# Two mixer blocks on one core: slab columns taken later and freed sooner, and four constants loaded into the slab for their stage

## The chip, the cores and the metric

The kernel runs on one core of a Trainium2 chip. The metric is the device time of one execution in microseconds (us). The engines are TensorE (PE in the profile, with its weight loads as PEld), VectorE (DVE), ScalarE (ACT), GpSimd (POOL) and SyncE (SP), which here only issues transfers. All run at the same time, each through its own instructions in a fixed order, and wait for one another on semaphores.

## What is computed

Two transformer blocks over 256 tokens of width 1024, in 32-bit floats. The part that matters here is the first block's mixer:

```python
hn = rms_norm(h, norm_mix_pre)
p = hn @ w_in                                   # 6912 columns
p_rw, p_ret, g_rw, g_ret = split(p)
y_rw  = rwkv7_mixer(p_rw, ...)                  # recurrence over the tokens, 8 heads of 64
y_ret = retention_mixer(p_ret, positions)       # 8 heads, decay mask, silu gate, group norm
merged = sigmoid(g_rw) * (y_rw @ w_branch_rw) + sigmoid(g_ret) * (y_ret @ w_branch_ret)
h = h + rms_norm(merged @ w_out, norm_mix_post)
```

After it come a convolutional feed-forward layer and the second block (a gated feed-forward layer, a gated mixer with a state-space branch, another feed-forward layer and an output gate).

## The kernel before, in words

**Weights.** All weights come as one stream of 335 chunks of 128 x 1024 floats (512 KB). A chunk is loaded by SP into one of six `stage` buffers, split by ACT into an f16 part (`hi`) and by DVE into the bf16 remainder (`lo`), and then used by PE in three products for each 128 x 128 tile (hi x hi, hi x lo, lo x hi). `take` (class `Stream`) loads five chunks and splits two chunks ahead of use. A chunk is 24 products of 256 columns, or 12 of 512 columns where the tokens are the stationary side (`token_major`). A product goes to a PSUM bank, `main` for the stream and `side` for the mixers' small products; the bank is free for the next tile when ACT or DVE has read it.

**The slab.** Everything else lives in one SBUF tensor, `slab`, of 32688 columns of 128 floats. `pr.buf(n)` takes n columns (class `Slab`), `.free()` gives them back. Columns that are given back are taken again later in the program, and then the new owner's first write must wait until the old owner's last reader or writer is done: a wait between two steps that have no data in common. `Slab.get` looks for a place whose old owner is done early, by the times of the plan's last round, and takes a later one where there is none.

**The order of the work.** The program is run once to record every operation with its operands (`Plan.add`, `Plan.touch`); a list scheduler (`Plan.run`) then gives each engine its order by its own prices, and `build` repeats this for four rounds and keeps the one with the shortest plan. `Plan.issue` emits the instructions in that order, so nearly all of them have line 484 in the profile. The order on each engine is fixed from then on: an instruction that waits holds up all that stand behind it on its engine.

**The first block's mixer.** `BlockOne.run` (lines 1539 to 1672) streams `w_in`: first the columns of RWKV, then retention's v, q and k, retention's gate (`RET_G`, four tiles of 512 columns, read from PSUM by `evac_g`, line 1517), and the two branch gates (16 tiles, `evac_gate`, line 1524). Beside it run two generators, `rwkv` (line 1059) and `retention` (line 1427), that hand in their small steps between the stream's tiles. `rwkv` builds decayed keys and queries for four tiles t, then

- writes the diagonal blocks of its triangular matrices to HBM and reads them back by rows into `lt` (lines 1225 to 1232),
- inverts them by forward substitution, 31 steps of two DVE operations on `x`, `tmp` and `lt` (lines 1246 to 1259),
- writes the result to HBM twice (`scr_g`, `scr_h`) and reads it back into `gb`, `hb` and `rb`, which must be zero elsewhere (lines 1222 to 1224 and 1260 to 1274),
- multiplies the blocks together (lines 1280 to 1304), solves for the state in two halves, and normalizes (lines 1307 to 1400).

`retention` works on four heads at a time (a quad): scores, decay mask, product with v, statistics; then the gate and eight transposes that give `y_ret`. The branches' products follow in the stream: `w_branch_ret` needs all of `y_ret`, `w_branch_rw` all of `y_rw`.

**The constants in question.** `w2a2` and `g2` (512 columns each, second half of `cst`), `sel8t` and `eye32` (512 each, in `konst`) are loaded at the start into tensors of their own and stay for the whole program. `decay` (3072 columns) and retention's v (`vrb`, 2048) are slab buffers, taken before retention begins and freed after it has ended.

Of the kernel before, what the change touches and what calls it, by code (L numbers as in the profile page):

```python
# [18 lines left out]
T = 256  # L19
# [29 lines left out]
SLAB = 32688  # L49
# [946 lines left out]
class BlockOne:  # L996
# [64 lines left out]
    def rwkv(self):  # L1061
# [3 lines left out]
        w2a2, g2 = pr.col("w2a2", 0, 512), pr.col("g2", 0, 512)  # L1065
# [36 lines left out]
        for t in range(4):  # L1102
# [31 lines left out]
            mm(bank[:, 0:T], lhsT=k_["sel8t"][:, t * P : t * P + P], rhs=rk.ap, start=True, stop=True)  # L1134
# [83 lines left out]
        rk.free()  # L1218
        self.wdad.free()


        gb, hb, rb = pr.buf(1024), pr.buf(2048), pr.buf(512)
        for b in (gb, rb, hb):
            pr.G.memset(b.ap, 0.0)
# [25 lines left out]
        V.tensor_copy(x.ap, k_["eye32"])  # L1250
# [8 lines left out]
        V.tensor_copy(tmp.v("p (c i) -> p i c", c=16), xv)  # L1259
        sg = pr.dram("scr_g", (2, 4, 16, 32, 16))  # L1260
        sh = pr.dram("scr_h", (2, 4, 16, 16, 32))
        pr.plan.sync.dma_start(out=sg.rearrange("a b h i c -> (a b h) (i c)"), in_=x.ap)
        pr.plan.sync.dma_start(out=sh.rearrange("a b h c i -> (a b h) (c i)"), in_=tmp.ap)
        hcs = lambda b: b.v("p (h n) -> p h n", h=16)
# [10 lines left out]
        for b in (lt, x, tmp):  # L1275
            b.free()
# [97 lines left out]
        for b in (u, ut, b2, state, hb, m4, r0, vt, bt, kt0, *self.AR, *self.F):  # L1374
            b.free()
        rs = pr.buf(16)
# [10 lines left out]
        for t in range(4):  # L1387
            bank = pr.bank()
            for c in range(2):
                pr.transpose(bank[:, c * P : c * P + P], ytv[:, c, t * P : t * P + P])  # L1390
            mm(bank[:, T : 2 * T], lhsT=g2[:, t * P : t * P + P], rhs=self.gd.ap, start=True, stop=True)
            o = pr.buf(T)
            S.activation(o.ap, bank[:, 0:T], AF.Identity, scale=pr.col("rw_lnx_w", t), bias=pr.col("rw_lnx_b", t))
            V.tensor_tensor(out=o.ap, in0=o.ap, in1=self.bv[t].ap, op=ADD)
            V.tensor_tensor(out=o.ap, in0=bank[:, T : 2 * T], in1=o.ap, op=MUL)
            self.bv[t].free()
            pr.unbank(bank)
            self.y_rw.append(pr.split(o.ap))
            o.free()
            yield  # L1400
        yt.free()
        self.gd.free()
# [25 lines left out]
    def retention(self):  # L1428
# [3 lines left out]
        for quad in range(2):  # L1432
# [5 lines left out]
            qs, kk = self.rot["q", quad], self.rot["k", quad]  # L1438
            for pair in range(2):
# [6 lines left out]
                for i, bank in enumerate(banks):  # L1446
                    h = 4 * quad + 2 * pair + i
                    s = pr.buf(384)
                    V.tensor_tensor(out=s.ap, in0=bank[:, 0 : 3 * P], in1=pr.k["decay"][:, 3 * P * h : 3 * P * h + 3 * P], op=MUL)
                    pr.unbank(bank)  # L1450
                    ss.append(s)
# [3 lines left out]
                for i, s in enumerate(ss):  # L1455
                    h = 4 * quad + 2 * pair + i
                    e = slice(P * i, P * i + P)
                    v0, v1 = self.vr[:, 0, h * P : h * P + P], self.vr[:, 1, h * P : h * P + P]
# [7 lines left out]
            for b in qs + kk:  # L1466
                b.free()
# [10 lines left out]
        self.vrb.free()  # L1478
# [34 lines left out]
    def evac_v(self, c, nh, ps):  # L1513
        self.pr.S.activation(self.vr[:, c, 512 * nh : 512 * nh + 512], ps, AF.Copy)
# [15 lines left out]
    def run(self):  # L1530
# [49 lines left out]
        dec = pr.buf(3072)  # L1580
        pr.plan.sync.dma_start(out=dec.ap, in_=pr.ins["decay"])
        pr.k["decay"] = dec.ap
        self.vrb = pr.buf(2048)
        self.vr = self.vrb.v("p (c n) -> p c n", c=2)
# [21 lines left out]
        dec.free()  # L1606
# [474 lines left out]
_KEEP = ("ones", "ident", "sel2", "sel8t", "inv", "mask", "blk64", "eye32")  # L2081


def build(tc, ins, out, at, at2):
    nc = tc.nc
    with tc.tile_pool(name="sb", bufs=1) as sb, \
# [7 lines left out]
        cst = sb.tile([P, ins["cst"].shape[1]], F32, name="cst")  # L2094
# [18 lines left out]
def program(pr, hall, kt):  # L2113
# [21 lines left out]
    load("sel2", "sel8t", "inv")  # L2135
    pr.plan.sync.dma_start(out=pr.cst[:, nv:], in_=ins["cst"][:, nv:])
    pr.ws.load_to(3)
    load("mask", "blk64", "eye32")
# [36 lines left out]
```

## Time and profile before

| | us |
|---|---|
| median of 3 runs (lowest, highest) | 1011.3 (1009.15, 1011.61) |
| the profiled execution | 1015.67 |
| its span, first to last instruction | 1013.9 |
| PE busy, PE idle in the span | 983.4, 30.5 |
| DVE busy | 794.5 |
| ACT busy | 613.8 |

The profiled execution is one run, 4.4 us above the median; the trace's times are counted from its first instruction. PE's granted clock is given as a share of 2.4 GHz: 1.00 is that level and 0.50 is 1.2 GHz. A pipelined product is shown longer than the step from one to the next (a product of 256 columns of f16 is shown with 270 ns), so where PE is full the records overlap and the busy time is that of their union. Since almost every instruction has line 484, groups are told apart by their operands: `lo<-stage,hi` is a split, `slab<-slab` on DVE with 496, 480, 464 ... columns is forward substitution, `slab<-main 128x512` on ACT is `evac_g` (or retention's v), `scr_l`, `scr_g` and `scr_h` are the three trips through HBM.

### The profile page before, as it was taken

The page shows a single profiled execution, that of the slowest core. Times are in us where ns is not written, and L with a number is a line of the kernel's source. Part 1 is how long each engine was busy: PE and PEld are TensorE (multiplying, and loading weights), DVE is VectorE, ACT ScalarE, POOL GpSimd, SP SyncE. Part 2 cuts the span into 40 slices and gives each one's busy share as a digit, 9 for nine tenths or more (in the row PEclk, how much of TensorE's full clock was granted, in tenths as well). Part 3 has the DMA queues.
Part 4 walks back from the last instruction along what each step waited for, and adds up shares of the span by engine and source line. Part 5 has one row for each costly group of instructions (what it writes and reads, how often), then busy time and mean ns, then how long its engine had stood idle before and what let it go on. Part 6 is the DMA issues. An engine that isn't in the chain of part 4 may idle for free.

```text
span 1013.9 us, 22086 instructions
## 1 busy us (share of the span) xinstructions
PE 983.4 (97%) x8884; PEld 830.6 (82%) x8899; DVE 794.5 (78%) x1515; ACT 613.8 (61%) x1042; POOL 34.6 (3%) x35
## 2 busy tenths in 40 slices
PE   8999996999998999999999999999999999999996
PEld 6766745998987888889888888768887888888884
DVE  7999698679888999756977756589798987776654
ACT  6774432545686877556655545577899665554543
POOL 2100000100001000000000000000000000000000
PEclk9899998999999999999999999999999999999999
DMA  9646656246636766664766666655545686666621
GB/s 344 233 150 197 183 166 194 74 155 224 204 96 220 218 203 204 204 197 140 236 204 204 200 198 205 198 179 161 198 124 173 201 273 205 202 196 205 198 75 42
DMA packets 60790, 189.68 MB, mean 187 GB/s; under 512 B 13184, under 2 KB 14992, under 8 KB 60176
## 3 DMA queue, kind: packets, MB, share of 16 engines
q1 hardware_dynamic: 59824, 185.39, 58.6%
q10 hardware_dynamic: 864, 2.89, 0.8%
q8 instruction: 69, 1.13, 0.5%
q14 instruction: 33, 0.27, 0.1%
HBM read 185.35 MB, written 1.85 MB: 185 GB/s over the span
## 4 chain that ended last, share of the span: by engine, by line
PE 71%; DVE 15%; ACT 6%; DMA 4%; issue 3%; POOL 1%; SPq 0%; POOLq 0%; ACTq 0%; DVEq 0%
PE main L484 44%; PE side L484 27%; DVE slab L484 11%; DVE lo L484 4%; ACT slab L484 3%; ACT hi L484 1%; DMA stage<-stream 1%; DMA slab<-scr_cs 1%; PE side L237 1%; DVE h L484 1%; POOL slab L484 1%; ACT L484 1%; DMA slab<-scr_l 1%; DMA h<-xt 1%; DMA scr_cs<-slab 0%
## 5 line engine op out<-in xcount | busy, mean ns | idle before, releaser
L484 PE MATMUL main<-slab,hi 128*128 128x256 f16 (+2 forms) x3276 | 553.7, 270 | 11.9 <-DVE slab L484 10.3
L484 PEld LDWEIGHTS <-hi 128*128 128x128 f16 x5080 | 489.3, 99 | 73.4 <-issue 13.3
L484 ACT ACTIVATE hi<-stage 128x1024 f16<-128x1024 f32 (+1 forms) x338 | 351.8, 1047 | 277.2 <-PE main L484 172.1
L484 DVE TENSOR_TENSOR lo<-stage,hi 128x1024 bf16<-128x1024 f32 (+1 forms) x338 | 406.8, 1210 | 139.3 <-ACT hi L484 138.5
L484 PE MATMUL main<-slab,lo 128*128 128x256 f16 (+1 forms) x1638 | 438.5, 272 | 0.4 <-DVE lo L484 0.4
L484 PE MATMUL side<-slab,hi 128*128 128x256 f16 (+3 forms) x1804 | 278.4, 260 | 2.0 <-DVE slab L484 1.1
L484 PEld LDWEIGHTS <-lo 128*128 128x128 bf16 x2540 | 249.2, 98 | 33.2 <-issue 3.7
L484 PE MATMUL side<-slab,lo 128*128 128x256 f16 (+1 forms) x902 | 225.3, 262 | 0.0
L484 DVE TENSOR_TENSOR slab<-slab 128x256 f32<-128x256 f32 (+13 forms) x427 | 165.5, 405 | 18.0 <-ACT slab L484 15.6
L484 ACT ACTIVATE slab<-slab 128x256 f32<-128x256 f32 (+4 forms) x302 | 116.7, 419 | 34.1 <-DVE slab L484 25.1
L484 PE MATMUL main<-hi,slab 128*128 128x512 f16 (+3 forms) x304 | 83.4, 357 | 0.6
L484 PEld LDWEIGHTS <-slab 128*128 128x128 f16 (+1 forms) x521 | 47.8, 101 | 42.6 <-issue 3.0
L484 ACT ACTIVATE slab<-side 128x128 f32<-128x128 f32 (+5 forms) x93 | 32.1, 379 | 51.8 <-PE side L484 42.5
L484 PEld LDWEIGHTS side<-slab 128*128 128x128 f32 x376 | 51.8, 192 | 8.4 <-DVE slab L484 4.4
L484 PE MATMUL side<-slab 128*128 128x64 f32 (+3 forms) x379 | 56.1, 264 | 2.5 <-DVE slab L484 2.3
L484 POOL TENSOR_TENSOR slab<-slab 128x2 f32<-128x2 f32 (+2 forms) x19 | 28.9, 1518 | 838.5 <-DVE slab L484 825.7
L484 PE MATMUL main<-lo,slab 128*128 128x512 bf16 (+3 forms) x138 | 48.5, 354 | 0.0
L484 DVE TENSOR_TENSOR slab<-side,slab 128x512 f32<-128x512 f32 (+4 forms) x58 | 32.7, 579 | 11.0 <-PE side L484 5.4
L484 DVE SCALAR_TENSOR_TENSOR slab<-main,cst,slab 128x255 f32<-128x255 f32 (+2 forms) x88 | 38.8, 469 | 1.6 <-ACT slab L484 1.5
L484 DVE SCALAR_TENSOR_TENSOR slab<-h,cst,slab 128x256 bf16<-128x256 f32 (+2 forms) x88 | 35.4, 427 | 2.3 <-ACT slab L484 2.2
L484 ACT ACTIVATE slab<-main 128x256 f32<-128x256 f32 (+2 forms) x66 | 25.3, 402 | 15.3 <-DMA scr_g<-slab 6.9
L484 DVE TENSOR_TENSOR slab<-main,slab 128x256 f32<-128x256 f32 (+1 forms) x53 | 28.6, 550 | 5.7 <-PE main L484 4.2
(60 smaller groups left out, 400.9 us busy)
## 6 DMA issues: line engine op xcount, KB each, us to landing
stage<-stream SPq DMA_DIRECT2D x332, 512.0 KB, 4.3
slab<-scr_cs SPq DMA_DIRECT2D x1, 2048.0 KB, 9.3
stage<-stream SPq DMA_DIRECT2D x6, 256.0 KB, 5.5
slab<-decay SPq DMA_DIRECT2D x1, 1536.0 KB, 8.4
slab<-slab SPq DMA_DIRECT2D x32, 32.0 KB, 1.9
slab<-last ACTq DMA_DIRECT2D x1, 1024.0 KB, 7.0
slab<-cst ACTq DMA_DIRECT2D x1, 1024.0 KB, 11.2
h<-xt SPq DMA_DIRECT2D x3, 256.0 KB, 6.1
```

What stands on the lines that cost most here:

```text
L237: op = self.new("PE", lambda: [fn(*args, **kw) for _, fn, args, kw in calls], (), {})
L484: o.fn(*o.args, **o.kw)
```

## The change

- The slab grows by 2048 columns to 34736, which are the columns of the four constants, no longer in `cst` and `konst`.
- `w2a2` and `sel8t` are loaded into slab buffers that `rwkv` takes as it begins and frees after its four tiles; `g2` into one that it takes near its end; `eye32` straight into `x`, in place of a DVE copy.
- `gb`, `hb` and `rb` (3584 columns) are taken after forward substitution instead of before it, and `lt` (1024) is freed before them instead of after.
- `decay` and v are held for each quad: two buffers of 1536 columns, taken as the quad begins, and two of 1024, each freed with its quad.

```diff
-SLAB = 32688
+SLAB = 34736
...
-        w2a2, g2 = pr.col("w2a2", 0, 512), pr.col("g2", 0, 512)
+
+        w2a2b, selb = pr.buf(512), pr.buf(512)
+        a = pr.at["w2a2"][0]
+        pr.plan.sync.dma_start(out=w2a2b.ap, in_=pr.ins["cst"][:, a : a + 512])
+        pr.plan.sync.dma_start(out=selb.ap, in_=pr.ins["sel8t"])
+        w2a2 = w2a2b.ap
...
-        rk.free()
+        for b in (rk, selb, w2a2b):
+            b.free()
         self.wdad.free()
-
-
-        gb, hb, rb = pr.buf(1024), pr.buf(2048), pr.buf(512)
-        for b in (gb, rb, hb):
-            pr.G.memset(b.ap, 0.0)
...
-        V.tensor_copy(x.ap, k_["eye32"])
+        pr.plan.sync.dma_start(out=x.ap, in_=pr.ins["eye32"])
         for j in range(31):
...
         V.tensor_copy(tmp.v("p (c i) -> p i c", c=16), xv)
+        lt.free()
         sg = pr.dram("scr_g", (2, 4, 16, 32, 16))
...
         pr.plan.sync.dma_start(out=sh.rearrange("a b h c i -> (a b h) (c i)"), in_=tmp.ap)
+
+
+        gb, hb, rb = pr.buf(1024), pr.buf(2048), pr.buf(512)
+        for b in (gb, rb, hb):
+            pr.G.memset(b.ap, 0.0)
...
-        for b in (lt, x, tmp):
+        for b in (x, tmp):
             b.free()
...
+        g2b = pr.buf(512)
+        a = pr.at["g2"][0]
+        pr.plan.sync.dma_start(out=g2b.ap, in_=pr.ins["cst"][:, a : a + 512])
         rs = pr.buf(16)
...
+            dec = pr.buf(1536)
+            pr.plan.sync.dma_start(out=dec.ap, in_=pr.ins["decay"][:, 1536 * quad : 1536 * quad + 1536])
             for pair in range(2):
...
-            for b in qs + kk:
+            for b in (*qs, *kk, dec, self.vrb[quad]):
                 b.free()
...
-        self.vrb.free()
...
-        dec = pr.buf(3072)
-        pr.plan.sync.dma_start(out=dec.ap, in_=pr.ins["decay"])
-        pr.k["decay"] = dec.ap
-        self.vrb = pr.buf(2048)
-        self.vr = self.vrb.v("p (c n) -> p c n", c=2)
+        self.vrb = [pr.buf(1024) for _ in range(2)]
+        self.vr = [b.v("p (c n) -> p c n", c=2) for b in self.vrb]
...
-_KEEP = ("ones", "ident", "sel2", "sel8t", "inv", "mask", "blk64", "eye32")
+_KEEP = ("ones", "ident", "sel2", "inv", "mask", "blk64")
...
-    load("sel2", "sel8t", "inv")
-    pr.plan.sync.dma_start(out=pr.cst[:, nv:], in_=ins["cst"][:, nv:])
+    load("sel2", "inv")
     pr.ws.load_to(3)
-    load("mask", "blk64", "eye32")
+    load("mask", "blk64")
```

Since the slab's places and the plan are made anew, the change moves instructions from about the 16th on DVE to the end of the first block's mixer, and a few behind it. Three places follow; `[waits ...]` names what an instruction waits for: an engine, or a transfer (`DMAHW0` to `DMAHW7`).

ACT, where the four tiles of retention's gate are read from PSUM (`slab<-main 128x512`; `128x256` are the branch gates, `hi` the splits, `128x2x256` retention's output). Before, from the first of the four tiles to the last:

```order
L484 ACTIVATE slab<-main_88 128x512 [waits PE_49]
L484 ACTIVATE hi_73<-stage_61 128x1024 [waits DMAHW5_49,PE_49]
L484 ACTIVATE slab<-main_85 128x512 [waits DMAHW7_49,DMAHW3_49,PE_49]
...
L484 ACTIVATE slab<-main_85 128x256 [waits DMAHW6_49,PE_49]
L484 ACTIVATE hi_73<-stage_64 128x1024 [waits DMAHW0_49]
L484 ACTIVATE slab<-main_86 128x512 [waits DMAHW4_49,DVE_49]
L484 ACTIVATE slab<-main_87 128x512 [waits DMAHW5_49]
L484 ACTIVATE slab<-slab 32x8x32 [waits DMAHW1_49,DMAHW0_49,Pool_49]
```

And now, the same four tiles:

```order
L484 ACTIVATE slab<-main_88 128x512 [waits PE_49]
L484 ACTIVATE hi_73<-stage_61 128x1024 [waits DMAHW5_49,PE_49,Activation_49]
L484 ACTIVATE slab<-side_92 128x2x256 [waits DVE_49,PE_49]
L484 ACTIVATE slab<-main_85 128x512 [waits PE_49]
L484 ACTIVATE hi_74<-stage_62 128x1024 [waits DMAHW4_49,PE_49,Activation_49]
L484 ACTIVATE hi_75<-stage_63 128x1024 [waits DMAHW7_49,DVE_49,PE_49]
L484 ACTIVATE hi_67<-stage_64 128x1024 [waits DMAHW1_49,DVE_49,PE_49]
L484 ACTIVATE slab<-main_86 128x512 [waits PE_49]
L484 ACTIVATE hi_68<-stage_65 128x1024 [waits DMAHW2_49,DVE_49,PE_49]
L484 ACTIVATE slab<-main_87 128x512 [waits PE_49]
```

Before, the third and fourth tile stand last before the copies of the inverted blocks (`32x8x32`), behind nine splits, and wait for transfers; now all four stand among the splits and wait for PE alone. The third and fourth buffer lay on `x` and on `tmp` before; now they lie on the first quad's half of `decay` and on columns that nobody needs.

SP, around the trip through `scr_l` (`slab<-slab 32x256` are the copies that put retention's q and k in order). Before, from the first write to the reads:

```order
L484 DMA scr_l<-slab 32x16x32
L484 DMA slab<-slab 32x256 x5
L484 DMA scr_l<-slab 32x16x32
L484 DMA slab<-slab 32x256 x3
L484 DMA stage_64<-stream 128x1024
L484 DMA scr_l<-slab 32x16x32
L484 DMA slab<-slab 32x256 x5
L484 DMA scr_l<-slab 32x16x32
L484 DMA slab<-slab 32x256 x3
L484 DMA stage_66<-stream 128x1024
L484 DMA slab<-scr_l 64x1024 x2
```

And now:

```order
L484 DMA scr_l<-slab 32x16x32 x2
L484 DMA stage_62<-stream 128x1024
L484 DMA scr_l<-slab 32x16x32
L484 DMA stage_63<-stream 128x1024
L484 DMA slab<-slab 32x256 x2
L484 DMA scr_l<-slab 32x16x32
L484 DMA slab<-slab 32x256 x4
L484 DMA slab<-scr_l 64x1024 x2
```

From the first write to the second of the two reads the queue goes 23 transfers on before, and 13 now.

SP at the start, where the constants are loaded. Before:

```order
L484 DMA stage_61<-stream 128x1024
L484 DMA cst<-cst 128x1024
L484 DMA konst<-sel8t 128x512
L484 DMA slab<-pos 128x256
L484 DMA stage_62<-stream 128x1024
...
L484 DMA konst<-eye 128x512
L484 DMA slab<-decay 128x3072
L484 DMA stage_63<-stream 128x1024
L484 DMA stage_64<-stream 128x1024
```

And now:

```order
L484 DMA slab<-cst 128x512
L484 DMA slab<-sel8t 128x512
L484 DMA konst<-sel 128x2
L484 DMA slab<-pos 128x256
L484 DMA stage_62<-stream 128x1024
...
L484 DMA slab<-decay 128x1536
L484 DMA slab<-eye 128x512
L484 DMA stage_63<-stream 128x1024
L484 DMA slab<-decay 128x1536
L484 DMA stage_64<-stream 128x1024
```

`w2a2`, `sel8t`, `eye32` and both halves of `decay` are still loaded at the start, into slab columns that are free then; only `g2` has gone (it comes after 39 chunks), and one half of `decay` has moved behind a chunk.

On PE, two numbers stand for the move: the first product after forward substitution (`side<-slab 128x64`, line 1287 before and 1294 now) comes after 884 products of the stream before, and after 1010 now, with the same small products ahead of it; and between the last product that makes `y_rw` and the first of `w_branch_rw` lie 152 products of `w_branch_ret` before, and 56 now. On DVE, the last step of forward substitution has 54 splits ahead of it before and 57 now, and two more products of retention's gate; the first quad's masks and statistics (7 operations) stand ahead of its first step before and among its steps now.

## Rows read from the trace of the kernel before

**Rows 1.** The page, part 1: busy time, share, instructions of each engine.

```profile
PE 983.4 (97%) x8884; PEld 830.6 (82%) x8899; DVE 794.5 (78%) x1515; ACT 613.8 (61%) x1042; POOL 34.6 (3%) x35
```

**Rows 2.** Busy time in stretches: us, busy (instructions) by engine, clock, DMA share, GB/s.

```profile
30.80:37.10 6.30, 6.25 (x33) 4.95 (x34) 6.06 (x14) 5.31 (x11) 2.95 (x1) 0.50 0.53 174
100.00:122.30 22.30, 22.10 (x177) 17.51 (x177) 12.82 (x25) 8.93 (x13) 0.00 (x0) 1.00 0.62 154
122.30:150.00 27.70, 26.62 (x144) 14.47 (x146) 27.66 (x51) 11.92 (x13) 0.00 (x0) 1.00 0.56 178
...
166.40:175.40 9.00, 0.04 (x1) 0.00 (x0) 6.20 (x17) 1.46 (x3) 0.96 (x1) 0.72 0.54 188
175.40:180.40 5.00, 4.93 (x23) 3.29 (x23) 0.69 (x1) 1.54 (x5) 0.00 (x0) 0.50 0.49 62
180.40:237.30 56.90, 55.90 (x537) 52.36 (x536) 41.55 (x121) 28.60 (x52) 6.63 (x2) 1.00 0.45 150
305.00:320.00 15.00, 11.66 (x93) 9.46 (x92) 12.64 (x23) 7.38 (x13) 3.82 (x1) 0.91 0.80 279
650.00:670.00 20.00, 19.89 (x97) 9.76 (x98) 12.63 (x21) 12.84 (x20) 0.70 (x1) 1.00 0.63 186
```

**Rows 3.** ACT in order of time: start, us, operation, [idle before <- what ended it].

```profile
162.07 0.37 ACT L484 ACTIVATE slab<-main 128x256 f32<-128x256 f32 x1
166.10 1.06 ACT L484 ACTIVATE hi<-stage 128x1024 f16<-128x1024 f32 x1 [3.67 <-DMA stage<-stream]
174.04 0.60 ACT L484 ACTIVATE slab<-main 128x512 f32<-128x512 f32 x1 [6.88 <-DMA scr_g<-slab]
175.29 0.60 ACT L484 ACTIVATE slab<-main 128x512 f32<-128x512 f32 x1 [0.65 <-DMA scr_h<-slab]
```

**Rows 4.** PE in order of time, the same columns.

```profile
175.41 0.58 PE L484 MATMUL main<-slab,hi 128*128 128x256 f16 x2 [8.97 <-DVE slab L484]
...
179.90 0.66 PE L484 MATMUL side<-slab 128*128 128x64 f32 x2
```

**Rows 5.** DVE in order of time, the end of forward substitution and after.

```profile
171.95 1.23 DVE L484 COPY slab<-slab 128x512 f32<-128x512 f32 x1
174.67 0.69 DVE L484 SCALAR_TENSOR_TENSOR slab<-slab,main 128x512 f32<-128x512 f32 x1 [1.49 <-ACT slab L484]
...
242.29 0.41 DVE L484 TENSOR_TENSOR slab<-slab 128x256 bf16<-128x256 f32 x1
```

**Rows 6.** The chain that ended last, in order of time: start, us, what.

```profile
115.49 6.83 DMA slab<-scr_l
122.34 6.96 DVE slab L484 x16
...
175.41 4.42 PE main L484 x20
...
237.27 27.07 PE main L484 x248
```

**Rows 7.** SP in order of time, the trip through scr_l.

```profile
100.11 0.42 SPq L484 DMA_DIRECT2D scr_l<-slab  x1
...
114.95 1.13 SPq L484 DMA_DIRECT2D slab<-scr_l  x2
```

**Rows 8.** DVE groups from 122.3 to 173.2: shapes, count, busy us, mean ns, idle before.

```profile
L484 DVE TENSOR_TENSOR lo<-stage,hi 128x1024 bf16<-128x1024 f32 x15 | 18.2, 1215 | 0.9 <-ACT hi L484 0.8
...
L484 DVE BATCH_NORM_STATS2 slab<-slab 128x6 f32<-128x128 f32 x8 | 2.2, 277 | 0.0
L484 DVE SCALAR_TENSOR_TENSOR slab<-slab,main 128x512 f32<-128x512 f32 x2 | 1.4, 677 | 0.0
...
L484 DVE TENSOR_TENSOR slab<-side,slab 128x384 f32<-128x384 f32 x2 | 1.1, 547 | 0.0
```

**Rows 9.** DVE groups from 40 to 122, the copy of eye32.

```profile
L484 DVE COPY slab<-konst 128x512 f32<-128x512 f32 x1 | 0.4, 418 | 0.0
```

More of the change, by code (lines that the diff above doesn't have):

```diff
@@ L1133, in rwkv @@
             bank = pr.bank()
-            mm(bank[:, 0:T], lhsT=k_["sel8t"][:, t * P : t * P + P], rhs=rk.ap, start=True, stop=True)
+            mm(bank[:, 0:T], lhsT=selb[:, t * P : t * P + P], rhs=rk.ap, start=True, stop=True)
             kk = pr.buf(T)
@@ L1390, in rwkv @@
                 pr.transpose(bank[:, c * P : c * P + P], ytv[:, c, t * P : t * P + P])
-            mm(bank[:, T : 2 * T], lhsT=g2[:, t * P : t * P + P], rhs=self.gd.ap, start=True, stop=True)
+            mm(bank[:, T : 2 * T], lhsT=g2b[:, t * P : t * P + P], rhs=self.gd.ap, start=True, stop=True)
             o = pr.buf(T)
@@ L1401, in rwkv @@
         yt.free()
+        g2b.free()
         self.gd.free()
@@ L1448, in retention @@
                     s = pr.buf(384)
-                    V.tensor_tensor(out=s.ap, in0=bank[:, 0 : 3 * P], in1=pr.k["decay"][:, 3 * P * h : 3 * P * h + 3 * P], op=MUL)
+                    d = 3 * P * (h % 4)
+                    V.tensor_tensor(out=s.ap, in0=bank[:, 0 : 3 * P], in1=dec[:, d : d + 3 * P], op=MUL)
                     pr.unbank(bank)
@@ L1457, in retention @@
                     e = slice(P * i, P * i + P)
-                    v0, v1 = self.vr[:, 0, h * P : h * P + P], self.vr[:, 1, h * P : h * P + P]
+                    d = slice(h % 4 * P, h % 4 * P + P)
+                    v0, v1 = self.vr[quad][:, 0, d], self.vr[quad][:, 1, d]
                     mm(pov[:, 0, e], lhsT=s[:, 0:P], rhs=v0, start=True, stop=True)
@@ L1513, in evac_v @@
     def evac_v(self, c, nh, ps):
-        self.pr.S.activation(self.vr[:, c, 512 * nh : 512 * nh + 512], ps, AF.Copy)
+        self.pr.S.activation(self.vr[nh][:, c, :], ps, AF.Copy)
     def evac_g(self, c, nh, ps):
@@ L1605, in run @@
         pr.finish(g_ret)
-        dec.free()
         def evac_ret(i, ps):
@@ L2093, in build @@
         hall = sb.tile([P, NK * T], F32, name="h")
-        cst = sb.tile([P, ins["cst"].shape[1]], F32, name="cst")
+        cst = sb.tile([P, at["end"][0]], F32, name="cst")
         kt = sb.tile([P, sum(ins[n].shape[1] for n in _KEEP)], F32, name="konst")
```

## The prediction

> **What bounds the kernel now.** I read the page first, for the share of each engine: PE is busy 983.4 of 1013.9 us [rows 1], so all that a reordering can give back is 30.5 us of idle PE, and what PE loses at its lower clock. The busy times in stretches then show where that is. From 166.4 to 175.4 PE does nothing, 9.0 us, and from 175.4 to 180.4 it works at clock 0.50, its 1.2 GHz level, after having stood still [rows 2]. At 1.00 those 5.0 us are 2.5, so this one place costs 11.5 us. No other comes near: 3.3 us are idle in 305 to 320, in the first block's last norm, which the change leaves alone, and 30.8 to 37.1 runs at 0.50 as well [rows 2].
>
> Engine by engine in order of time, the wait reads backwards. PE's next product waits 8.97 us for DVE [rows 4]: the bank it writes holds a gate tile, which DVE reads last, at 174.67 [rows 5]. DVE waited for ACT's read of the same tile, and ACT waited 6.88 us, until 174.04, for the transfer `scr_g<-slab` [rows 3]. A gate tile has no data from RWKV. It waits because its 512 columns are those of `x`, which forward substitution writes until 171.95 and the transfer then reads; the fourth tile waits likewise for `tmp` (`scr_h`) [rows 3, 5]. Both wait for old owners of slab columns.
>
> **What the change does there.** It makes room just then: 2048 columns from the constants, 1536 from half of `decay`, 3584 from `gb`, `hb` and `rb`, which no longer lie idle through forward substitution. In the new order the four gate tiles stand among the splits and wait for PE alone. So that wait goes: 9.0 us, and 2.5 us of slow clock.
>
> **What is late next.** Forward substitution itself is no shorter. PE now meets it later, at the first block product, 126 products of the stream further on. In the old order 20 products lay between the wait and that product [rows 6]. At 27.07 / 248 = 0.109 us a product [rows 6] PE comes there at 166.4 + 146 x 0.109 = 182.3.
>
> When are the blocks there? The start is the landing of `lt`. Its trip went from 100.11 to the second read at 115.49, 23 transfers or 0.67 us each, and that read took 6.83 us [rows 6, 7]. With 13 transfers it is issued at 100.1 + 8.7 = 108.8 and lands at 115.6, not 122.3. From there DVE took 49.6 us to 171.95 [rows 5, 6]. The new order puts more among the steps: three splits (3 x 1.215 = 3.6), two gate products (2 x 0.677 = 1.4), the first quad's four masks and three statistics (4 x 0.547 + 3 x 0.277 = 3.0) [rows 8]. That makes 57.6 us, so the end is at 173.2. From the last step to the first block product it was 8.0 us, 171.95 to 179.90 [rows 4, 5]: the blocks are there at 181.2, 1.1 us before PE. If `lt` lands no earlier than it did, they come at 187.9 and PE waits 5.6 us. So this term lies between 0 and -5.6 us, and with it perhaps the slow clock again. I take 0, since DVE had nothing to do for 9.5 of the 22.3 us before 122.3 [rows 2] and the shorter queue is in the order, not in a guess.
>
> **The smaller terms.** In 122.3 to 150, where DVE is full, PE lost 1.1 us in 27.7 [rows 2]; DVE is now full 8.0 us longer: -0.3. In 180.4 to 237.3 PE lost 1.0 us in steps that wait for small results [rows 2]. There the cover shrinks, since PE has used up the branch gates earlier: `w_branch_ret` starts right after the first transposes, and behind the last product of `y_rw` lie 56 products, 6.1 us, where 152 lay. The last split of `y_rw` ended 5.4 us after that point, at 242.7 [rows 5, 6], so it is still covered, by 0.7 us; I charge the same 1.0 us again (bounds 0 and 3.0). The loads of `w2a2`, `sel8t`, `eye32` and `decay` stay in the burst at the start, and no step waits for them; if one did, PE would lose what the first stretch leaves to lose, a microsecond or so. `g2` comes after 39 chunks, long before its use. The copy of `eye32` on DVE (0.4 us [rows 9]) goes and is not on the path: it ran while `lt` was still to come. The `ob` memset on POOL moves to the start, off every path.
>
> **Sum.** 9.0 + 2.5 - 0.3 - 1.0 = 10.2 us less: the profiled execution's 1015.67 becomes 1005.5. That execution lies 4.4 us above the median of the runs, and a wait on the chain is the same length in both, so I take 1011.3 - 10.2 = **1001.1 us**.
>
> **The rivals.**
>
> *A. The wait moves to the first block product.* `lt` lands as late as before and the longer DVE work does the rest. For it: by the sum above PE has only 1.1 us to spare, and PE takes its products in a fixed order, so every microsecond that the blocks are late is lost. Against it: the idle DVE before 122.3 and the shorter queue on SP. It gives back 5.6 + 2.5, so 1009.2. In milder form it is half of that, and still faster.
>
> *B. DVE is the bound of the stretch, not the slab.* DVE is busy 27.66 of 27.70 us from 122.3 to 150 [rows 2]; if it also sets PE's pace until 173, the idle time of PE is only cut into pieces, and the kernel takes 1011.3 + 1.3 = 1012.6. The Trainium skill, in Perfetto Trace Analysis, Identifying the Most-Contended Engine, says that matmul busy time does not tell how near PE is to its limit, and to take the busy share of its weight loads instead. By that rule PE has room in this stretch, since its loads are busy 14.47 of 27.70 us, 52% [rows 2], DVE is the engine to relieve, and the time is this rival's. The rows speak against reading the rule so: from 650 to 670, with DVE at 63% and PE never short of work, the loads are busy just 9.76 of 20 us, 49% [rows 2], because a product of 512 columns needs half as many loads, and the stretch from 122.3 is made of such products. So I leave B little.
>
> *C. Slower: DVE's own queue holds forward substitution up.* The new order sets the first quad's masks between the first steps. They wait for scores, and these for q and k, whose last copies are on SP behind the reads of `lt`. DVE stops at a mask that is not ready, the steps behind it too, and on ACT the copies of the inverted blocks then hold up the splits behind them, so that PE starves. It decides from the point where the blocks come after 193.0: PE waits 10.7 us, 2.5 more go to the clock, and the 10.2 won are lost with 3.0 on top. That takes an `lt` no earlier than before and another 5.1 us on DVE. I put it at 1016. Against it: at 0.67 us a copy the ten copies behind `lt` are issued by 115.6, as the first step begins.
>
> *D. The slow stretch at the start goes too.* From 30.8 to 37.1 PE ran at 0.50 after short pauses; the new order has other pauses there. Without the 3.2 us that this costs, and with the 1.3 us above not charged, it is 996.6. For it only that the order changed; DVE's work there has not become less.
>
> **How the numbers follow.** The forecast 0.72, A 0.11, B 0.06, C 0.04, D 0.07. About 0.3%, 3.0 us, is what a measurement of this kernel can tell from no change, so faster means under 1008.3 and slower over 1014.3. Faster: the forecast, D and the milder half of A, 0.84. Same: the rest of A and most of B, 0.11. Slower: C and a little of B, 0.05. The range reaches from D with a microsecond more for the start, 995.5, to just below A, 1008.5; A in full, B and C are left out.
>
> **What would show it.** Right: no wait of ACT for `scr_g` before a gate tile, no idle time of PE over 3 us between 120 and 240, the clock at 1.00 through that stretch, `lt` landed by about 116, PE's idle time near 21 us in all. The first block product comes at about 182. Wrong: PE idle by several microseconds just before that product (A), or small waits for splits all through 120 to 170 (B), or idle time of DVE between steps of forward substitution (C).

## The result and the profile after

The changed kernel takes 1001.25 us (median of 6 runs, 1000.02 to 1005.39), the kernel before beside it 1010.22 (6 runs, 1008.98 to 1013.0): a ratio of 0.9915, 95% interval 0.9892 to 0.9938. Forecast were 1001.1 and a gain. The profiled execution took 1001.03, with a span of 999.1 us at a mean clock of 0.994; that of before took 1015.67, so the two profiles lie further apart than the medians, which is taken up below. A ratio in this document leaves out an execution that took over 1.5% more than the fastest of its kernel; there is one, the 1018.07 us of e5, which its median and range keep.

The page of the changed kernel, part 1, answers [rows 1]: 22.9 us of idle PE in 999.1, where 30.5 were.

```profile
PE 976.2 (98%) x8899; PEld 829.0 (83%) x8899; DVE 794.0 (79%) x1514; ACT 608.3 (61%) x1038; POOL 33.1 (3%) x35
```

Its stretches (us, PE, PEld, DVE, ACT and POOL busy, clock, DMA share, GB/s), cut at its own places, answer [rows 2]: the start, the time before `lt` lands, forward substitution in two parts, the wait for the blocks, the chain behind them.

```profile
28.60:35.40 6.80, 6.32 (x34) 4.88 (x34) 6.76 (x14) 4.85 (x11) 2.49 (x1) 0.50 0.68 248
100.00:114.70 14.70, 14.70 (x138) 13.28 (x137) 10.39 (x17) 6.59 (x10) 0.00 (x0) 1.00 0.65 164
114.70:150.00 35.30, 34.70 (x220) 21.46 (x218) 35.16 (x63) 14.63 (x18) 0.00 (x0) 1.00 0.64 208
150.00:171.30 21.30, 21.30 (x198) 18.96 (x196) 20.51 (x63) 10.63 (x16) 0.00 (x0) 1.00 0.67 205
179.50:181.00 1.50, 0.14 (x2) 0.09 (x1) 0.65 (x1) 0.82 (x1) 0.00 (x0) 1.00 0.69 85
181.00:237.30 56.30, 54.50 (x519) 51.16 (x520) 42.63 (x128) 25.53 (x47) 5.79 (x2) 1.00 0.42 130
```

The stall of 9.0 us is gone and the clock stays at 1.00 from 100 to 237. ACT reads the third gate tile as soon as PE has written it and the fourth right behind a split, 22 to 24 us before forward substitution ends at 171.04 (ACT in order of time, as [rows 3]):

```profile
147.21 0.60 ACT L484 ACTIVATE slab<-main 128x512 f32<-128x512 f32 x1 [1.10 <-PE main L484]
...
148.65 0.59 ACT L484 ACTIVATE slab<-main 128x512 f32<-128x512 f32 x1
```

Forward substitution's first and last step on DVE, as [rows 5]:

```profile
114.82 0.68 DVE L484 TENSOR_TENSOR slab<-slab 128x496 f32<-128x496 f32 x1 [1.16 <-DMA slab<-scr_l]
...
171.04 0.61 DVE L484 COPY slab<-slab 128x512 f32<-128x512 f32 x1
```

PE at the first block products, as [rows 4]. It now waits there, 1.36 us, and then sets one product of the stream behind each of the first block products, which have two records each (further on there are short groups without the stream, the longest of 26 records):

```profile
180.91 0.43 PE L484 MATMUL side<-slab 128*128 128x64 f32 x2 [1.36 <-DMA slab<-scr_g]
181.19 0.27 PE L484 MATMUL main<-slab,lo 128*128 128x256 f16 x1
181.29 0.33 PE L484 MATMUL side<-slab 128*128 128x64 f32 x2
181.46 0.27 PE L484 MATMUL main<-slab,hi 128*128 128x256 f16 x1
```

The chain that ended last, as [rows 6], shows what stands between the last step and that product: the store of `scr_h` (5.60 us), and behind it on SP the reads of `scr_g` that the first block product needs.

```profile
110.61 4.13 DMA slab<-scr_l
...
114.82 4.20 DVE slab L484 x9
...
171.68 5.60 DMA scr_h<-slab
...
177.29 0.30 SPq L484
...
177.65 0.44 SPq L484
...
178.14 2.73 DMA slab<-scr_g
```

**The 14.8 us between the two profiled spans.** Here a span is split into PE's idle time, half of the time that PE is busy at 0.50, and what is left: PE's work as it would take at full clock. Added up from the clock of the stretches and PE's records (every execution also holds some 4 to 6 us at 0.50 at the very end, but PE's last product is over by then, so they belong to the idle time):

| profile | span | PE idle | PE busy at 0.50 | what is left |
|---|---|---|---|---|
| before | 1013.9 | 30.5 | 15.1 | 975.8 |
| before, again (e10) | 1008.9 | 30.3 | 6.9 | 975.1 |
| changed | 999.1 | 22.9 | 6.3 | 973.1 |
| changed, again (e12) | 998.4 | 21.7 | 6.8 | 973.3 |
| e2 | 1014.9 | 22.5 | 32.5 | 976.1 |
| e2's order again (e11) | 1007.7 | 26.0 | 12.1 | 975.6 |

So some 7.6 us of the 14.8 are idle time, 4.4 are clock, and 2.7 stand in the last column: PE's own work, of which the prediction has no term. Against e10, an execution of before nearer to its median, e12 gains 8.6 us of idle time, nothing by the clock and 1.8 in the last column. Which products take less time was not traced.

### The profile page after: what moved, and what is told of

It reads as the page before. It is cut to its first block, busy times and chain, and to the rows that moved or that the text cites. A ratio compares the mean times of both kernels' runs of the same rounds, so it can differ in the third digit from the quotient of the medians.

```text
span 999.1 us, 22098 instructions
## 1 busy us (share of the span) xinstructions
PE 976.2 (98%) x8899; PEld 829.0 (83%) x8899; DVE 794.0 (79%) x1514; ACT 608.3 (61%) x1038; POOL 33.1 (3%) x35
## 4 chain that ended last, share of the span: by engine, by line
PE 82%; DVE 8%; DMA 4%; ACT 3%; issue 2%; SPq 1%; POOL 0%; POOLq 0%; ACTq 0%; DVEq 0%
PE main L484 51%; PE side L484 29%; DVE slab L484 6%; DVE lo L484 2%; ACT slab L484 2%; PE side L237 1%; DMA slab<-scr_cs 1%; ACT hi L484 1%; DMA slab<-cst 1%; DVE h L484 1%; DMA scr_h<-slab 1%; SPq L484 1%; DMA h<-xt 1%; DMA stage<-stream 0%; POOL slab L484 0%
## 5 line engine op out<-in xcount | busy, mean ns | idle before, releaser
L484 PEld LDWEIGHTS <-lo 128*128 128x128 bf16 x2540 | 249.5, 98 | 30.5 <-issue 2.8
L484 ACT ACTIVATE slab<-slab 128x256 f32<-128x256 f32 (+3 forms) x302 | 117.0, 419 | 30.2 <-DVE slab L484 23.7
L484 PE MATMUL side<-slab 128*128 128x64 f32 (+3 forms) x396 | 60.3, 269 | 3.3 <-DVE slab L484 1.8
L484 PEld LDWEIGHTS side<-slab 128*128 128x128 f32 x392 | 53.8, 191 | 9.3 <-DVE slab L484 3.9
L484 PE MATMUL main<-lo,slab 128*128 128x512 bf16 (+3 forms) x152 | 53.8, 356 | 0.0
L484 PE MATMUL side<-konst,slab 128*128 128x128 f32 (+3 forms) x160 | 28.1, 262 | 2.9 <-DVE slab L484 1.5
```

Source lines behind the costliest of these rows:

```text
L484: o.fn(*o.args, **o.kw)
```

## The experiments

Theory 1 was the prediction's: gate tiles waited for old owners of their columns, and any edit that gives them other columns takes the wait away. Theory 2 was that the shorter lifetimes do it and the constants are a side matter; theory 3, that the order came out better somewhere else. After e1 to e4 a clock theory stood beside them: small f32 products that run bare, with none of the stream between them, bring PE's clock down. All results, each against the kernel before on the same chip:

| run | median us | lowest to highest (runs) | ratio, 95% interval |
|---|---|---|---|
| changed | 1001.25 | 1000.02 to 1005.39 (6) | 0.9915, 0.9892 to 0.9938 |
| e1 constants only | 1002.43 | 1000.23 to 1004.30 (4) | 0.9917, 0.9888 to 0.9945 |
| e2 lifetimes only | 1014.20 | 1004.57 to 1018.08 (10) | 1.0012, 0.9981 to 1.0044 |
| e3 gb, hb, rb late only | 1021.55 | 1018.77 to 1024.08 (4) | 1.0102, 1.0075 to 1.0128 |
| e4 gate tiles on x, tmp | 1002.50 | 1001.48 to 1006.85 (4) | 0.9922, 0.9894 to 0.9950 |
| e5 no alternation | 1009.26 | 1002.11 to 1018.07 (10) | 0.9985, 0.9953 to 1.0016 |
| e6 without quads | 1003.87 | 999.91 to 1007.08 (8) | 0.9929, 0.9906 to 0.9952 |
| e7 lt, second trip | 1006.73 | 1003.33 to 1009.83 (10) | 0.9968, 0.9947 to 0.9988 |
| e8 quads only | 1003.05 | 1001.57 to 1007.37 (7) | 0.9934, 0.9909 to 0.9959 |
| e9 branch gates late | 1013.65 | 1007.51 to 1021.07 (10) | 1.0036, 1.0005 to 1.0066 |

**e1, the constants alone** (on the kernel before):

```diff
-SLAB = 32688
+SLAB = 34736
...
+        w2a2b, selb = pr.buf(512), pr.buf(512)
...
-        V.tensor_copy(x.ap, k_["eye32"])
+        pr.plan.sync.dma_start(out=x.ap, in_=pr.ins["eye32"])
```

> Only the constants move into the slab (2048 columns more); `gb`, `hb`, `rb` are taken early, `lt` is freed late, `decay` and the values of retention stay whole, as before. In this order none of the four gate tiles has an old owner that ends later than 131, and 1028 products of the stream stand ahead of the first block product. Theory 1 (the old owners of the gate tiles were the cost, whichever edit frees room): 1001, within 3; no wait of ACT for scr_g ahead of a gate tile, no idle time of PE over 3 us between 120 and 240, clock 1.00 there. Theory 2 (the shorter lifetimes do it, the constants are a side matter): 1010, with an ACT wait of 5 us or more ahead of a gate tile. Theory 3 (a chance of the new order at the start or in the first block's norm): no tie to the gate tiles, anything from 999 to 1010.

1002.43: theory 1's number, not theory 2's. One detail was missed. The four gate tiles are free, but three of the sixteen *branch* gate tiles, which come next, lie on `x` and `tmp`, and ACT waits for `scr_g` before those; PE loses 2.27 us there (ACT, then PE, in order of time):

```profile
177.82 1.01 ACT L484 ACTIVATE slab<-main 128x256 f32<-128x256 f32 x3 [3.48 <-DMA scr_g<-slab]
```

```profile
178.26 0.38 PE L484 MATMUL main<-slab,hi 128*128 128x256 f16 x2 [2.27 <-ACT slab L484]
```

This profile has no slow stretch at its start at all, and its execution took as long as the changed kernel's (1001.02 against 1001.03), with 1.8 us more of idle PE. `lt` is early here too: forward substitution begins at 110.73. So e1 does not tell free columns from an early `lt`.

**e2, the lifetimes alone** (on the kernel before: the diff's edits of `lt`, `gb`, `hb`, `rb`, `decay` and the values, without those of e1).

> Only the lifetimes change (`lt` freed earlier, `gb`, `hb`, `rb` later, `decay` and values per quad); the constants and the slab are those of before. In this order the first three gate tiles stand free; the fourth lies on the first 512 columns of `lt`, free after step 16 of 31 of forward substitution. In the changed kernel that step ended at 151.2 and the fourth tile was read at 148.65. Theory 1: one wait of ACT of 2 to 5 us, ended by DVE and not by a transfer; 1001 to 1005. Theory 2 (lifetimes do it): 1001. If only the 2048 columns of the constants count: 1010.

The waits came as expected or shorter: ACT waits for DVE no longer than 1.62 us up to the fourth tile, PE is idle for 0.96 us before the first block product and nowhere longer than that from 120 to 240. The time did not: 1014.20. PE and the stretch behind that product show why (PE in order of time; the stretch has the columns of [rows 2]):

```profile
181.29 3.78 PE L484 MATMUL side<-slab 128*128 128x64 f32 x28 [0.96 <-DMA slab<-scr_g]
185.00 1.65 PE L237 MATMUL side<-slab 64*128 64x256 f32 x8
186.59 17.66 PE L484 MATMUL side<-slab 128*128 128x32 f32 x80
```

```profile
184.00:214.70 30.70, 29.12 (x136) 28.00 (x136) 13.42 (x45) 5.52 (x12) 2.90 (x1) 0.50 0.17 64
```

The block products run bare, with nothing of the stream between them, and the clock is at 0.50 for 30.7 us. In the order of e2 the four gate tiles have free columns or early ones, but four branch gates lie on columns that are given up only when retention's output has been gated or `scr_h` stored. ACT reads branch gates at 187.81, after a wait for DVE, and then none until 210.78, after another; a tile that is not read holds its bank, PE takes its products in a fixed order, and so it has only block products left:

```profile
187.81 0.66 ACT L484 ACTIVATE slab<-main 128x256 f32<-128x256 f32 x2 [1.19 <-DVE slab L484]
...
210.78 0.66 ACT L484 ACTIVATE slab<-main 128x256 f32<-128x256 f32 x2 [5.90 <-DVE slab L484]
```

**e3, gb, hb, rb late alone** (on the kernel before: the three buffers taken after the stores of `scr_g` and `scr_h`, nothing else).

> Of the whole change only `gb`, `hb` and `rb` are taken later: 3584 columns freed, more than the 2048 of the constants. In this order the third gate tile lies on columns of `tmp` and of a score product, the fourth on `rb`, which the block products read last, behind forward substitution; 888 products of the stream stand ahead of the first block product. Theory 1 (not the amount of room counts but whose columns the gate tiles get): no gain, 1009 to 1016, PE idle for 6 us or more around 166 to 180, slow clock after it. Rival (room is room: the gain goes with the columns freed): 1001 or less.

1021.55, slower than before by 0.75% at least, in spite of 3584 columns more and of forward substitution that begins at 115.87. Theory 1's sign held and its range, 1009 to 1016, was too low: the idle time of 7.30 us is followed by bare block products, and the clock stays at 0.50 for 27.3 us, where in the kernel before it was back within a microsecond of the first block product, which there alternates with the stream [rows 2, 4].

```profile
174.52 5.78 PE L484 MATMUL side<-slab 128*128 128x64 f32 x26 [7.30 <-DMA slab<-scr_g]
```

```profile
172.30:199.60 27.30, 24.15 (x116) 22.99 (x117) 9.94 (x35) 6.08 (x14) 3.41 (x2) 0.50 0.07 10
```

**e4, the wait put back** (on the changed kernel):

```diff
-        for b in (x, tmp):
-            b.free()
+        self.old = [x, tmp]
...
-        b = pr.buf(512)
+        b = self.old.pop(0) if len(self.gs) >= 2 else pr.buf(512)
```

> The changed kernel with one thing put back: the third and fourth gate tile are set onto the columns of `x` and `tmp`. `lt` lands as early as in the changed kernel; 908 products of the stream stand ahead of the first block product, 15 splits instead of 19 lie among the steps of forward substitution, which so ends at about 165. Theory 1: the wait is back, but shorter than in the kernel before, since `lt` is early: PE is idle 3 us ahead of the gate tiles and 3 us more ahead of the first block product, 1007 (1004 to 1010). Theory 3 (the gain comes from the order elsewhere) or the early `lt` alone: 1001.

1002.50, below theory 1's 1004 to 1010 and nearer to the 1001 of its rivals (the order elsewhere, or the early `lt` alone): this is the run that corrects the prediction most. ACT does wait for `scr_g` again, and PE is idle for 3.9 us and slow for 3.0 more:

```profile
167.42 1.17 ACT L484 ACTIVATE slab<-main 128x512 f32<-128x512 f32 x2 [2.09 <-DMA scr_g<-slab]
```

```profile
164.90:168.80 3.90, 0.02 (x2) 0.01 (x1) 0.75 (x2) 1.55 (x3) 0.00 (x0) 0.94 0.65 200
168.80:171.80 3.00, 3.00 (x15) 2.08 (x15) 0.54 (x1) 0.66 (x2) 0.00 (x0) 0.50 0.53 62
171.80:215.00 43.20, 41.95 (x413) 39.69 (x412) 33.52 (x84) 23.21 (x43) 2.90 (x1) 1.00 0.52 164
```

That is 3.9 + 1.5 = 5.4 us, not 9.0 + 2.5. `lt` lands at 113.6 here, and forward substitution with fewer splits among its steps ends 7.3 us sooner than in the changed kernel (copy at 163.79 against 171.04). The blocks start at 173.32 instead of 180.91, and PE loses 1.25 us from 171.8 to 215 and none from there to 240, where the changed kernel loses 1.36 at the blocks and 1.80 behind them. Of the 5.4 us some 1.2 are left in the median, which its interval does not tell from nothing.

**e5, no alternation in the first block** (on the changed kernel; the flag by which the scheduler puts something else between two small f32 products is off there):

```diff
...
-                op.tiny = n <= 64
+                op.tiny = n <= 64 and self.alt
...
```

> The changed kernel, but in the first block the order no longer sets a product of the stream between two small f32 products. The gate tiles stand free as in the changed kernel, and 1076 products of the stream stand ahead of the first block product, so PE does not wait there; but the block products then run in groups of 31, 16, 8, 8 and 22 instead of one at a time. In run e2 72 of them ran back to back and the clock was 0.50 for 30.7 us, in e3 40 of them and 27.3 us; where they alternate with the stream the clock stayed at 1.00. Clock theory (bare block products bring the clock down): a stretch at 0.50 of 10 to 30 us within 185 to 225, so 5 to 15 us lost, 1006 to 1016. Rival (the slow clock of e2 and e3 came from the short idle time ahead of the block products, or by chance): clock 1.00 there, 1000 to 1003.

Neither side cleanly. The ten executions go from 1002.11, at a mean clock of 0.995, to 1018.07, at 0.982. The one under the profile took 1003.17, and its stretch from 187 to 215 is at 1.00:

```profile
187.00:215.00 28.00, 26.44 (x234) 25.28 (x235) 17.58 (x53) 10.28 (x24) 2.90 (x1) 1.00 0.30 91
```

So bare groups of this length, up to 68 records here, don't always bring the clock down. That they did so in the longer executions fits the mean clock, but where the clock was low in those was not recorded.

This profile shows something else. `lt` lands as late as before, and still PE waits only 1.39 us at the first block product and is idle 20.0 us in all, less than in the changed kernel (DVE's first step, then PE's first block products):

```profile
123.25 2.08 DVE L485 TENSOR_TENSOR slab<-slab 128x496 f32<-128x496 f32 x3 [1.77 <-DMA slab<-scr_l]
```

```profile
187.91 3.31 PE L485 MATMUL side<-slab 128*128 128x64 f32 x28 [1.39 <-issue]
```

With free columns and 1076 products of the stream ahead of that point, a late `lt` brought no more idle time.

**e6, without the quads, and e8, the quads alone** (the diff's edits of `decay` and the values, taken out of the changed kernel and put alone into the one before).

> The changed kernel with `decay` and the values of retention whole again (constants in the slab, `lt`, `gb`, `hb`, `rb` as changed). All four gate tiles stand free in this order, 1005 products of the stream stand ahead of the first block product, and block products alternate with the stream from the first on. Theory 1 with the clock theory: as the changed kernel, 1001 within 3, no stretch at 0.50 between 120 and 240. If the quads carry a part of the gain: 1004 or more.

> Of the whole change only `decay` and the values per quad: 1536 and 1024 columns freed early. In this order the first three gate tiles stand free and the fourth lies on columns of `lt` that the last steps of forward substitution read; 967 products of the stream stand ahead of the first block product, and block products alternate with the stream. Theory 1 with the clock theory: one wait of ACT that ends with forward substitution, 2 to 4 us before the landing of scr_g would have ended it, PE idle 2 to 6 us; 1003 to 1008, between before and the changed kernel. If what matters is only how much room there is: as e2's best, or 1001.

1003.87 and 1003.05, neither told apart from the changed kernel. e6 lies at the upper edge of theory 1's range and 0.13 us under the 1004 that was to speak for the quads, so it leaves open whether they carry a small part. `lt` is early in both (first steps at 111.61 and 115.69). In e6 the clock was at 0.50 for 3.4 us from 182 on, which its expectation had excluded. In e8 a branch gate waits for `scr_g`, as in e1, and the idle time of 1.57 + 1.98 us and 3.4 us at 0.50 cost 5.2 at that place:

```profile
175.47 0.38 ACT L484 ACTIVATE slab<-main 128x256 f32<-128x256 f32 x1 [5.11 <-DMA scr_g<-slab]
```

**e7, `lt` late** (on the changed kernel):

```diff
+        l0 = pr.buf(1024)
...
+        again = pr.dram("scr_l2", (P, 1024))
+        pr.plan.sync.dma_start(out=again, in_=l0.ap)
         lt = pr.buf(1024)
...
+        pr.plan.sync.dma_start(out=lt.ap, in_=again)
+        l0.free()
```

> The changed kernel, but `lt` makes a second trip through DRAM before it is used. By the first trip's rows (store to landing 3 to 4 us, read 4.1 us, two issues) it lands about 8 us later, at 123. The order sets 48 more products of the stream ahead of the first block product (1058), 5.2 us. If forward substitution's end sets when the block products start, as the prediction has it: PE waits 1.4 + 8 - 5.2 = 4 us there, and the cover behind the block products is 48 products smaller, so 1004 to 1008. If the landing of `lt` is not on the path: 1001.

1006.73, in the range, 5.5 us above the changed kernel: in this order the landing of `lt` is on the path. The wait at the block product is shorter than worked out, 2.12 us instead of 4 (DVE's first step, then PE's first block product), only 0.8 more than in the changed kernel. The rest is the thinner cover behind it: waits for DVE of 1.58 and 1.15 us, and the clock, 3.4 us at 0.50 from 187.5 and 6.8 from 208, the second over a group of 72 f32 records with none of the stream among them. e5 shows that another order can cover an `lt` as late as this.

```profile
123.09 0.68 DVE L484 TENSOR_TENSOR slab<-slab 128x496 f32<-128x496 f32 x1 [0.39 <-DMA slab<-scr_l]
```

```profile
187.30 0.47 PE L484 MATMUL side<-slab 128*128 128x64 f32 x2 [2.12 <-DMA slab<-scr_h]
...
210.06 6.20 PE L484 MATMUL side<-slab 128*128 128x128 f32 x33 [1.15 <-DVE slab L484]
```

```profile
208.00:214.80 6.80, 5.65 (x27) 5.46 (x27) 6.09 (x14) 0.00 (x0) 0.00 (x0) 0.50 0.60 209
```

**e9, branch gates late** (on the changed kernel; `self.old` holds the halves of two retention gate tiles, given up when they have been read):

```diff
...
-        b = pr.buf(T)
+        late = i in (6, 7) if out is self.th_ret else i in (2, 3)
+        b = self.old.pop(0) if late else pr.buf(T)
```

> The changed kernel with four of the sixteen branch-gate tiles (numbers 7 and 8 of the retention branch, 3 and 4 of the RWKV branch) set onto the columns of two retention gate tiles, which are read last when retention's output is gated. The four gate tiles themselves stand free as in the changed kernel. 1004 products of the stream stand ahead of the first block product; then 4 block products alternate with the stream and 59 run bare, because all banks hold branch gates that wait. Theory (e2's loss is the same wait one place later: branch gates on late columns hold the banks, the block products run bare, and the clock falls): a stretch at 0.50 of 10 us or more after 180 in most executions, median 1006 to 1016, executions spread over 8 us or more as in e2 and e5. Rival (e2's slow clock has to do with something else of its order): 1001 to 1003, spread as the changed kernel's, 5 us.

1013.65, spread over 13.6 us: the loss of e2, made in the changed kernel by four tiles of 256 columns. PE has 1.5 us of idle time before the block products and 1.31 among them; the slow stretch follows.

```profile
190.60 8.78 PE L485 MATMUL side<-slab 128*128 128x32 f32 x48 [1.31 <-ACT slab L485]
```

```profile
192.50:206.20 13.70, 12.97 (x62) 12.06 (x62) 8.21 (x23) 2.32 (x5) 2.19 (x1) 0.50 0.07 19
```

**e10, e11, e12: three orders a second time.**

> The kernel before, once more under the profile. If the profile before was 4.4 us above its median because the clock happened to be slow in more places (from 317 on, for one), this profile shows the idle time of 9 us at 166 again and fewer or other stretches at 0.50: span near 1009. If the extra time belongs to the program: 1013 again, with the same stretches.

> The kernel of e2 once more under the profile. The order is the same; if the slow clock behind the bare block products is what spreads its times from 1004.6 to 1018.1, this profile's time and the length of its stretch at 0.50 after 180 move together: about half a microsecond more time for each microsecond at 0.50 (e2: 30.7 us and 1016.9). If its waits spread the times, the stretch is as long again whatever the time.

> The changed kernel once more under the profile: block products alternate with the stream, so no long stretch at 0.50 between 120 and 240 (none, or one of 3.4 us), 1000 to 1004.

e10: the stall again, 8.62 us, with 3.5 us of slow work behind it, and no slow stretch from 305 to 320. The first profile's extra time was not the program's.

```profile
173.35 0.59 PE L484 MATMUL main<-slab,hi 128*128 128x256 f16 x2 [8.62 <-DVE slab L484]
```

```profile
173.30:176.80 3.50, 3.45 (x17) 2.39 (x17) 0.69 (x1) 1.23 (x3) 0.00 (x0) 0.50 0.52 60
305.00:320.00 15.00, 12.31 (x109) 10.46 (x108) 13.29 (x25) 8.86 (x17) 3.82 (x1) 1.00 0.64 227
```

e11: the order of e2, 1009.72 with one slow stretch of 13.7 us, where e2 had 1016.91 with 30.7. The same products in the same order run at 1.00 for longer (the first 32 records of 32 columns in 3.84 us) and begin to be slow later:

```profile
181.63 3.31 PE L484 MATMUL side<-slab 128*128 128x64 f32 x28 [0.98 <-DMA slab<-scr_g]
...
185.72 3.84 PE L484 MATMUL side<-slab 128*128 128x32 f32 x32
189.98 7.66 PE L484 MATMUL side<-slab 128*128 128x32 f32 x48 [0.42 <-ACT slab L484]
```

```profile
193.10:206.80 13.70, 12.11 (x57) 11.77 (x57) 6.87 (x21) 2.32 (x5) 2.41 (x1) 0.50 0.00 0
```

17.0 us less at 0.50 behind the blocks and 7.2 us less time, although e11 has 3.5 us more of idle PE: not far from half a microsecond for each. e12: 1000.32, the clock at 1.00 from 120 to 240, 3.4 us at 0.50 at the start where the first profile had 6.8, and 3.4 in the first block's norm, where the first profile of before had some and that of the changed kernel had none.

## Why the prediction came out right

- **"So that wait goes: 9.0 us, and 2.5 us of slow clock."** It went, and on the profile nothing else of that size did. But the step puts all of it down to the columns, and e4 contradicts that: with the columns as they were and `lt` early, the wait costs 5.4 us on the spot and 1.2, unresolved, in the end. Its length was that of a forward substitution begun at 122.3. The two causes, set side by side: free columns and early `lt` 1001.25, old columns and early `lt` 1002.50 (e4), free columns and late `lt` 1006.73 (e7), neither 1010.22. The change has both. The split between them is not clean, since every variant is an order of its own: e1, e6 and e8 have an early `lt` as well, and the profile of e5, with free columns and a late `lt`, has no more idle time than the changed kernel. Why the scheduler set fewer transfers ahead of the read was not traced; all variants but e7, which has a second trip, have 11 to 19 there.
- **The number.** 1001.1 against 1001.25 is closer than the sum deserves. It took 10.2 us from 1011.3, the median of three runs; measured were 9.0 us less than 1010.22. In the profiles, too, the terms differ: against e10 the clock gave back nothing in all, since the changed kernel's second execution is slow for 3.4 us elsewhere, and 1.8 us came from PE's own work, which stands in no term.
- **`lt` at 115.6.** 114.74 (the read took 4.13 us, not 6.83). Forward substitution took 56.2 us from first step to copy, where 57.6 were forecast.
- **"From the last step to the first block product it was 8.0 us."** This term was too small: 171.04 to 180.91 is 9.9. The third and fourth read of `scr_g` stand on SP behind a read that waits for the store of `scr_h`, and that store took 5.60 us.
- **"PE comes there at 182.3."** It came at 179.5. In e10 the stall itself begins 1.7 us earlier than in the first profile of before, so most of this is the execution; 0.7 us is that PE loses 0.6 us from 100 to 171 where it lost 1.3 from 100 to 166 [rows 2]. PE came 2.8 us sooner than forecast and the blocks only 0.3, which turns the slack of 1.1 us into a wait of 1.36, the mildest form of rival A.
- **-0.3 and -1.0.** The first became a small gain. The second was 1.8 in 181 to 237.3, within its bounds; the largest piece is a wait of 1.46 us for DVE at 213.9.
- **Rival B.** DVE is busy 35.16 of 35.30 us from 114.7 and the weight loads 61%, and PE still loses only 0.6: the busy share that the Trainium skill (Perfetto Trace Analysis, Identifying the Most-Contended Engine) puts forward would have named DVE here, and the measurement does not bear it out.
- **Rival C.** Nothing of it: from 114.8 to 171 the longest that DVE stood still is 0.28 us. Another way to become slower did exist, seen in e3, e2 and e9, and was not among the rivals: the prediction looked for waits and took the clock to follow from idle time alone.
- **Rival D.** It did not come: 28.6 to 35.4 is at 0.50 in the changed kernel as well. Whether its 3.2 us could be had stays open. The profiles of e1 and e4 have no slow stretch there and are no faster, but they have 1.8 and 1.1 us more of idle time. In e12, of the same order as the changed kernel, the stretch is half as long and forward substitution begins 0.7 us sooner, at 114.08.
- **What was to be seen.** No wait for `scr_g` before a gate tile, no idle time over 3 us, clock 1.00, `lt` by 116: all four. The first block product came at 180.9 instead of 182, and the idle time is 22.9 us instead of 21.

The expectations for e1, e6, e7, e8 and e9 held in their times, and so did those for e10, e11 and e12, with one execution each; those for e2 and e4 did not, e5's was left undecided, and e3's was too low.

## What to carry to other kernels

A stall at a reused buffer has two ends: whose columns the tile gets, and how late the old owner is done. Price each by undoing it alone, since they share one saving, and remember that each undoing makes a new order with other cover. And when room is freed, see which tile waits next: a tile that waits holds its bank, and what PE does meanwhile can cost more, by its clock, than the wait (30.7 us at 0.50 in e2, behind 0.96 us of waiting).

## What the runs showed of the hardware

- **The clock fell without idle time of PE worth the name.** In e2 PE had been busy 59.88 of 60 us up to 180, was idle for 0.96 us, ran small f32 products bare, and was at 0.50 from 184.0 to 214.7. In e11 and e9 it was 13.7 us. In PE's order, the longest group of f32 records with none of the stream among them has 150 records in e2 and e11, 124 in e9, 86 in e3 and 72 in e7, and PE is at 0.50 during part or all of each; in e3 the clock fell in the 7.30 us of idle time just before. Where the stream stands between most of them, with groups of 16 to 42 records at most, the clock held through the groups (the changed kernel, e1, e4, e6, e8); in e6 and e7 it was low for 3.4 us at the first block products, behind waits of 1.98 and 2.12 us. That the bare products are the cause is shown as far as e9 goes, which made the changed kernel run them bare and got the slow stretch; e5's profile, with a group of 68 at 1.00, shows that they need not do it. The Trainium skill, TensorE: Matmul & The Clock Gate, HAM oscillation, tells of this loss as one of PE's waits for data. Here PE's records, whose ends are modelled, show it busy 29.12 of those 30.70 us, so in this case the measurement goes against a clock that falls by waits for data alone.
- **The same order gives different times.** Ten executions each of three orders with bare groups spread over 13.5 (e2), 16.0 (e5; 11.6 without its longest) and 13.6 us (e9). The orders that alternate spread over 4 to 7.2 us in 4 to 10 executions, and e7, with ten, over 6.5. e3 is an exception, 5.3 us, but has only four. One execution of such a kernel tells little.
- **Alternating is cheap in itself.** A block product and a stream product together take 0.28 us (the changed kernel's start at 181.29, 181.57, 181.85 and so on), a bare block product at 1.00 takes 0.24 (e11: 28 records in 3.31 us). So the stream product costs 0.04 there, where it costs 0.109 alone [rows 6]. That fits e5, for which the last column of the table of spans would be 979.6, 6.5 more than for the changed kernel.
